# Moving the sink addition and the reciprocal of the softmax sums from VectorE to GpSimd

## The chip, the cores and the metric

The kernel runs on one core of a Trainium2 chip. The metric is device time in microseconds (us) from one launch; lower is better. A core has TensorE (PE; its weight loads are shown apart, as PEld), VectorE (DVE), ScalarE (ACT), GpSimd (POOL) and SyncE (SP), which here only issues DMAs. Each engine works through its own list of instructions in order, and waits at the head of the list for semaphores that other engines raise.

## The reference

Two layers over 512 tokens of width 1024. Each layer normalises its input, projects it, runs two branches and projects back. One branch is a gated linear recurrence (HGRN2), the other a sliding-window attention of 16 heads with a learned sink per head. Only the softmax of the attention matters here:

```python
s = jnp.where(mask, q_k_scores * ATT_SCALE, NEG_INF)        # (heads, 128 queries, 256 keys)
sink = broadcast(sinks)                                     # one logit more per head
p = jax.nn.softmax(jnp.concatenate([s, sink], axis=-1), axis=-1)[..., :-1]
o = jnp.einsum('bnkgqs,bnskd->bnqkgd', p, vw)
```

The sink's exponential therefore enters the sum that divides each row, and nothing else.

## The kernel before, in words

The work of a layer is a long list of projections (line L302: each 128x512 product is made of three matmuls, from a high and a low part of activations and weights), and beside them the attention and the recurrence. Weights arrive by DMA as `raw`; ACT copies out the high part (L189) and DVE subtracts it to get the low part `wlo` (L190).

The attention of a layer is 16 steps, one for each block `n` of 128 queries (4) and each group `g` of four heads (4). `att_stream` starts in turn i the scores of step i (`att_scores`), the transposes of step i-2 (`att_transpose`), and the products with V of step i-4 (`att_value`). `merge` interleaves these turns with projection steps in the text of the program. In a step:

- PE makes the scores into PSUM (`sc`, L560 for n = 0, L573 otherwise). DVE masks them (L564, L578), takes the row maximum (L566, L580), and forms the negated bound `negm` (L584) and the sink's exponent `ds` (L587).
- ACT takes four exponentials of 128x128 into `pt` (tile `s`), and accumulates each row's sum into a column of `sums`, 128x4 (L591). It then takes the exponential of the sink, `es`, 128x4 (L594).
- DVE adds `es` to `sums` (L595) and takes the reciprocal in place (L596).
- GpSimd multiplies the 128x512 tile `pt` by the reciprocals (L598).
- Two turns later PE transposes `pt` (L604). ACT and DVE split the transposes into a high and a low part in tile `a` (L350, L351). For n > 0 GpSimd cuts the two halves of the window out of them with two affine selects (L616, tiles `pcur` or `b`, and `pprev`). PE multiplies with V (L630), ACT and DVE fold the result (L632, L636).

GpSimd has other work in the same stretch: the last rotations of q (L524, L525) at its start, and the memset and products of the recurrence's preparation (L725, L743) at its end.

The order of the instructions on each engine is fixed when the program is built. Instructions given to `pin` keep the order of the text among themselves; scores, transposes and V products are pinned. All others, the projections' matmuls (L302) of this stretch and the instructions of DVE, ACT and GpSimd in `att_scores` among them, are ordered by a list scheduler with its own estimate of times. A few DVE instructions are raised by `tc.high_priority(300)`: mask, maximum, `negm` and `ds`. The addition and the reciprocal are not raised.

GpSimd already takes powers elsewhere: `rstd_of` computes an inverse square root of a 128x4 tile by a one-input addition (L355) and a power with a tile of -0.5, `mhalf` (L357); `power` does so for 128x1 (L371), and the start of the kernel once for `rcol` (L1180, L1181).

Of the kernel before, what the change touches and what calls it, by code (L numbers as in the profile page):

```python
# [10 lines left out]
F32 = mybir.dt.float32  # L11
# [3 lines left out]
ALU = mybir.AluOpType  # L15
# [62 lines left out]
def hybrid_kernel(ctx: ExitStack, tc: tile.TileContext, x, xt, wkv, win, wout, g_pre, g_post, lbp, ghead, sinks,  # L78
                  gcol_c, cos_f, sin_f, cos_t, sin_t, masks_c, out):
    nc = tc.nc  # L80
    P = 128
    const = ctx.enter_context(tc.tile_pool(name="const", bufs=1))
# [8 lines left out]
    def pin(ins):  # L91
        return tc.keep_in_program_order(ins)
# [8 lines left out]
    def sc():  # L101
        sc_turn[0] += 1
        return sc_tiles[sc_turn[0] % SC]
# [5 lines left out]
    def tmp(tag, dt=F32, n=1):  # L109

        t = tp.tile([P, n, 512] if n > 1 else [P, 512], dt, tag=tag, name=tag, bufs=TB[tag])
        return t
# [316 lines left out]
    def layer(l, last):  # L429
# [119 lines left out]
        def att_scores(g, n):  # L549
            v = g // 2  # L550
            q = qs[g]
            hs = slice(4 * g, 4 * g + 4)
            t_ = slice(n * P, (n + 1) * P)
            mx_ = sm.tile([P, 4], F32, tag="mx", name="mx")
            cur = []
            if n == 0:
                S = sc()
                for h in range(4):
                    for p in range(2):
                        pin(nc.tensor.matmul(S[:, h * P:(h + 1) * P], lhsT=q[:, h, t_], rhs=kst[v][p][:, 0:P],  # L560
                                         start=(h == 0 and p == 0), stop=(h == 3 and p == 1)))
                Sv = S.rearrange("p (h s) -> p h s", h=4)
                with tc.high_priority(300):
                    nc.vector.copy_predicated(Sv, am4, neg.unsqueeze(2).broadcast_to([P, 4, P]))  # L564
                with tc.high_priority(300):
                    nc.vector.tensor_reduce(mx_, Sv, axis=AX.X, op=ALU.max)  # L566
                cur = [Sv[:, h, :] for h in range(4)]
            else:
                for hp_ in range(2):
                    S = sc()  # L570
                    for h in range(2):
                        for p in range(2):
                            pin(nc.tensor.matmul(S[:, h * 256:(h + 1) * 256], lhsT=q[:, 2 * hp_ + h, t_],  # L573
                                             rhs=kst[v][p][:, (n - 1) * P:(n + 1) * P],
                                             start=(h == 0 and p == 0), stop=(h == 1 and p == 1)))
                    Sv = S.rearrange("p (h s) -> p h s", h=2)
                    with tc.high_priority(300):
                        nc.vector.copy_predicated(Sv[:, :, P:2 * P], am2, Sv[:, :, 0:P])  # L578
                    with tc.high_priority(300):
                        nc.vector.tensor_reduce(mx_[:, 2 * hp_:2 * hp_ + 2], Sv[:, :, P:2 * P], axis=AX.X, op=ALU.max)  # L580
                    cur += [Sv[:, h, P:2 * P] for h in range(2)]
            negm = sm.tile([P, 4], F32, tag="negm", name="negm")
            with tc.high_priority(300):
                nc.vector.scalar_tensor_tensor(negm, mx_, -SCALE, nsnk[:, l, hs], op0=ALU.mult, op1=ALU.min)  # L584
            ds_ = sm.tile([P, 4], F32, tag="ds", name="ds")
            with tc.high_priority(300):
                nc.vector.tensor_tensor(ds_, snk[:, l, hs], negm, op=ALU.add)  # L587
            pt = tmp("s")
            sums = sm.tile([P, 4], F32, tag="sums", name="sums")
            for h in range(4):  # L590
                nc.scalar.activation(pt[:, h * P:(h + 1) * P], cur[h], AF.Exp, bias=negm[:, h:h + 1], scale=SCALE,  # L591
                                     accum_out=sums[:, h:h + 1])
            es = sm.tile([P, 4], F32, tag="es", name="es")
            nc.scalar.activation(es, ds_, AF.Exp)  # L594
            nc.vector.tensor_tensor(sums, sums, es, op=ALU.add)  # L595
            nc.vector.reciprocal(sums, sums)  # L596
            pv = pt.rearrange("p (h s) -> p h s", h=4)
            nc.gpsimd.tensor_tensor(pv, pv, sums.unsqueeze(2).broadcast_to([P, 4, P]), op=ALU.mult)  # L598
            return pt
# [38 lines left out]
        def att_stream(steps):  # L638


            pts, terms = {}, {}
            n = len(steps)
            for tt in range(NT):
                ensure(("k", l, tt))
            for i in range(n + VLAG):
                todo = []
                if i < n:
                    todo.append(lambda: pts.update({i: att_scores(*steps[i])}))
                if 2 <= i <= n + 1:
                    todo.append(lambda: terms.update({i - 2: att_transpose(*steps[i - 2], pts.pop(i - 2), i % 2)}))  # L650
                if i >= VLAG:
                    todo.append(lambda: att_value(*steps[i - VLAG], terms.pop(i - VLAG)))
                for fn in todo:
                    fn()
                    yield (SLOW[1] if i < SLOW[0] else 1.0) / len(todo)

                if i < n and steps[i][1] == NT - 1 and steps[i][0] < 2:
                    until(lambda: steps[i][0] + 2 in stacks)
                    load_q(steps[i][0] + 2)
# [442 lines left out]
    nc.gpsimd.affine_select(out=ident, in_=ident, pattern=[[-1, P]], compare_op=ALU.is_equal, fill=0.0, base=0, channel_multiplier=1)  # L1102
    mhalf = const.tile([P, 4], F32, name="mhalf")
    nc.vector.memset(mhalf, -0.5)
    first = sm.tile([P, 4], F32, tag="hr", name="first")
    nc.scalar.activation(first, mhalf, AF.Square)
    ones = tmp("u")
# [207 lines left out]
```

## Time and profile before

| | |
|---|---|
| median of 3 runs | 903.64 us (903.24 to 903.84) |
| the profiled execution | 904.02 us |
| its span, first to last instruction | 902.3 us |
| busy: PE, PEld, DVE, ACT, POOL | 99%, 83%, 72%, 52%, 28% |
| attention of the first layer | about 58 to 166 us |
| attention of the second layer | about 500 to 610 us |

In the lines of the profile, "out<-in" names the tiles an instruction writes and reads. A group's line gives the count, the busy time and the mean duration in ns, and then the idle time of its engine just before it with what ended it. A row of the timeline gives start and duration in us, engine, line, operation and tiles, and in square brackets the idle time before it and its releaser. A row of the waits reads "who <- whom: us in total, times, longest".

### The profile page before, as it was taken

The page shows a single profiled execution, that of the slowest core. Times are in us where ns is not written, and L with a number is a line of the kernel's source. Part 1 is how long each engine was busy: PE and PEld are TensorE (multiplying, and loading weights), DVE is VectorE, ACT ScalarE, POOL GpSimd, SP SyncE. Part 2 cuts the span into 40 slices and gives each one's busy share as a digit, 9 for nine tenths or more (in the row PEclk, how much of TensorE's full clock was granted, in tenths as well). Part 3 has the DMA queues.
Part 4 walks back from the last instruction along what each step waited for, and adds up shares of the span by engine and source line. Part 5 has one row for each costly group of instructions (what it writes and reads, how often), then busy time and mean ns, then how long its engine had stood idle before and what let it go on. Part 6 is the DMA issues. An engine that isn't in the chain of part 4 may idle for free.

```text
span 902.3 us, 18581 instructions
## 1 busy us (share of the span) xinstructions
PE 893.0 (99%) x7206; PEld 747.7 (83%) x7206; DVE 650.7 (72%) x1179; ACT 472.3 (52%) x1067; POOL 256.5 (28%) x233
## 2 busy tenths in 40 slices
PE   9999999999999999999999999999999999999996
PEld 7888888888888888888898888888888888888885
DVE  5888987989666785555777787877767558666556
ACT  6536767754665323534464376686356463145242
POOL 0135445204313123021332344450124121330102
PEclk9999999999999999999999999999999999999999
DMA  9683712322222222434347455222322322223413
GB/s 307 222 225 117 211 46 72 105 94 80 77 82 70 94 82 63 128 119 132 116 153 217 128 164 163 71 80 76 115 72 61 105 71 86 70 73 93 140 36 140
DMA packets 57144, 102.82 MB, mean 114 GB/s; under 512 B 6624, under 2 KB 9184, under 8 KB 57056
## 3 DMA queue, kind: packets, MB, share of 16 engines
q1 hardware_dynamic: 56768, 101.50, 37.2%
q8 instruction: 57, 0.93, 0.4%
q14 instruction: 31, 0.25, 0.1%
q10 hardware_dynamic: 288, 0.14, 0.1%
HBM read 89.03 MB, written 12.58 MB: 113 GB/s over the span
## 4 chain that ended last, share of the span: by engine, by line
PE 95%; DVE 3%; ACT 1%; issue 0%; POOL 0%; POOLq 0%; DVEq 0%; ACTq 0%
PE pj L302 77%; PE ac L630 3%; PE sc L573 2%; PE sc L771 2%; PE ac L840 2%; PE ac L1140 1%; PE sc L604 1%; PE ac L843 1%; PE ac L827 1%; PE sc L902 1%; PE sc L815 1%; PE ac L712 1%; PE sc L560 1%; PE sc L1117 1%; DVE wlo L190 0%; PE sc L775 0%
## 5 line engine op out<-in xcount | busy, mean ns | idle before, releaser
L189 ACT CAST whi<-raw 128x512 fp32r<-128x512 f32 x256 | 155.5, 621 | 126.9 <-PE pj L302 113.4
L190 DVE TENSOR_TENSOR wlo<-raw,whi 128x512 fp32r<-128x512 f32 x253 | 184.1, 746 | 43.4 <-ACT whi L189 42.3
L302 PE MATMUL pj<-hhi,wlo 128*128 128x512 f32 x512 | 202.4, 396 | 0.0
L302 PE MATMUL pj<-hhi,whi 128*128 128x512 f32 x512 | 199.9, 390 | 0.0
L302 PE MATMUL pj<-hlo,whi 128*128 128x512 f32 x512 | 199.4, 389 | 0.0
L302 PE MATMUL pj<-whi,ops 128*128 128x512 f32 (+1 forms) x520 | 172.1, 395 | 0.0
L302 PEld LDWEIGHTS pj<-whi,ops 128*128 128x128 f32 x520 | 97.2, 188 | 19.6 <-DVE y L925 0.3
L302 PEld LDWEIGHTS pj<-hhi,whi 128*128 128x128 f32 x512 | 96.1, 188 | 20.6
L302 PEld LDWEIGHTS pj<-hhi,wlo 128*128 128x128 f32 x512 | 96.2, 188 | 19.3
L302 PEld LDWEIGHTS pj<-hlo,whi 128*128 128x128 f32 x512 | 96.3, 188 | 18.9
L302 PE MATMUL pj<-whi,hlo 128*128 128x512 f32 x256 | 102.9, 404 | 0.0
L302 PE MATMUL pj<-wlo,ops 128*128 128x512 f32 (+1 forms) x260 | 100.7, 387 | 0.0
L302 PE MATMUL pj<-wlo,hhi 128*128 128x512 f32 x256 | 100.1, 391 | 0.3 <-DVE wlo L190 0.3
L302 PE MATMUL pj<-whi,hhi 128*128 128x512 f32 x256 | 100.2, 391 | 0.0
L790 POOL TENSOR_TENSOR k<-k,tot 128x512 f32<-128x512 f32 x40 | 58.0, 1473 | 107.5 <-PE sc L771 51.8
L591 ACT ACTIVATE s<-sc,negm 128x128 f32<-128x128 f32 x128 | 45.6, 370 | 33.4 <-DVE negm L584 25.7
L302 PEld LDWEIGHTS pj<-whi,hhi 128*128 128x128 f32 x256 | 48.0, 188 | 10.3
L302 PEld LDWEIGHTS pj<-wlo,ops 128*128 128x128 f32 x260 | 49.0, 188 | 8.8
L302 PEld LDWEIGHTS pj<-wlo,hhi 128*128 128x128 f32 x256 | 48.3, 189 | 8.7 <-DVE wlo L190 0.8
L302 PEld LDWEIGHTS pj<-whi,hlo 128*128 128x128 f32 x256 | 48.2, 188 | 8.0
L789 DVE TENSOR_TENSOR q<-q,tot 128x512 f32<-128x512 f32 x40 | 37.6, 951 | 20.4 <-PE sc L775 10.9
L598 POOL TENSOR_TENSOR s<-s,sums 128x512 f32<-128x512 f32 x32 | 34.7, 1084 | 52.6 <-DVE sums L596 32.2
(223 smaller groups left out, 1391.4 us busy)
## 6 DMA issues: line engine op xcount, KB each, us to landing
raw<-in_win_dram SPq DMA_DIRECT2D x192, 256.0 KB, 2.7
raw<-in_wout_dram SPq DMA_DIRECT2D x64, 256.0 KB, 2.7
stack<-rot SPq DMA_DIRECT2D x16, 512.0 KB, 3.9
qs<-stack SPq DMA_DIRECT2D x32, 256.0 KB, 4.4
xs<-in_xt_dram SPq DMA_DIRECT2D x8, 256.0 KB, 4.8
raw<-in_wkv_dram SPq DMA_DIRECT2D x8, 256.0 KB, 3.7
a<-in_x_dram SPq DMA_DIRECT2D x8, 256.0 KB, 3.3
x_mid<-a SPq DMA_DIRECT2D x8, 256.0 KB, 2.2
```

Source lines behind the costliest of these rows:

```text
L189: keep(nc.scalar.copy(hi, v))
L190: keep((nc.gpsimd if i in on_pool and i % 2 else nc.vector).tensor_tensor(lo, v, hi.bitcast(F32), op=ALU.subtract))
L302: ins = nc.tensor.matmul(u.o, lhsT=u.sta(k, u.w)[i], rhs=u.mov(k, u.w)[j], start=(n == 0), stop=(n == len(u.list) - 1))
L560: pin(nc.tensor.matmul(S[:, h * P:(h + 1) * P], lhsT=q[:, h, t_], rhs=kst[v][p][:, 0:P], start=(h == 0 and p == 0), stop=(h == 3 and p == 1)))
L573: pin(nc.tensor.matmul(S[:, h * 256:(h + 1) * 256], lhsT=q[:, 2 * hp_ + h, t_], rhs=kst[v][p][:, (n - 1) * P:(n + 1) * P], start=(h == 0 a ...
L591: nc.scalar.activation(pt[:, h * P:(h + 1) * P], cur[h], AF.Exp, bias=negm[:, h:h + 1], scale=SCALE, accum_out=sums[:, h:h + 1])
L598: nc.gpsimd.tensor_tensor(pv, pv, sums.unsqueeze(2).broadcast_to([P, 4, P]), op=ALU.mult)
L630: pin(nc.tensor.matmul(U, lhsT=vst[v][:, blk, :], rhs=d, start=(i == 0), stop=(i == len(terms) - 1)))
L771: pin(nc.tensor.matmul(L[32 * b:32 * b + 32, c:c + 16], lhsT=k[:, o_ + 32 * b:o_ + 32 * b + 32], rhs=qv[:, blk:blk + qu, 1, :], start=True ...
L789: nc.vector.tensor_tensor(qv[:, :, 1, :], qv[:, :, 1, :], tv[:, :, 0].unsqueeze(2).broadcast_to([P, 2 * nb, hh]), op=ALU.mult)
L790: nc.gpsimd.tensor_tensor(kv_[:, :, 0, :], kv_[:, :, 0, :], tv[:, :, 1].unsqueeze(2).broadcast_to([P, 2 * nb, hh]), op=ALU.mult)
L840: pin(nc.tensor.matmul(O[:, c], lhsT=A[:, c], rhs=vs(j, n), start=(n == 0), stop=False))
```

## The change

The addition of the sink's exponential moves from DVE to GpSimd. The reciprocal becomes a power with an exponent of -1 on GpSimd, with the exponent read from a new constant tile `mone` of 128x4. Both stand directly ahead of GpSimd's scaling of the same step. The constant is filled once by GpSimd, right after the making of the identity at the start of the kernel.

```diff
             nc.scalar.activation(es, ds_, AF.Exp)
-            nc.vector.tensor_tensor(sums, sums, es, op=ALU.add)
-            nc.vector.reciprocal(sums, sums)
+            nc.gpsimd.tensor_tensor(sums, sums, es, op=ALU.add)
+            nc.gpsimd.tensor_tensor(sums, sums, mone, op=ALU.pow)
             pv = pt.rearrange("p (h s) -> p h s", h=4)
             nc.gpsimd.tensor_tensor(pv, pv, sums.unsqueeze(2).broadcast_to([P, 4, P]), op=ALU.mult)
...
     nc.vector.memset(mhalf, -0.5)
+    mone = const.tile([P, 4], F32, name="mone")
+    nc.gpsimd.memset(mone, -1.0)
```

## The prediction

> **What bounds the kernel now.** I read the page from the top first: span, busy shares, and the chain that ended last.
>
> ```profile
> span 902.3 us, 18581 instructions
> PE 893.0 (99%) x7206; PEld 747.7 (83%) x7206; DVE 650.7 (72%) x1179; ACT 472.3 (52%) x1067; POOL 256.5 (28%) x233
> PE 95%; DVE 3%; ACT 1%; issue 0%; POOL 0%; POOLq 0%; DVEq 0%; ACTq 0%
> ```
>
> PE is busy for 893.0 of 902.3 us, and 95% of the chain is its own work. GpSimd has no share of it. So time can be won only from PE's few gaps, and lost only where something makes PE wait longer. Next, the two stretches that hold all 32 attention steps, and the busiest part of the first one for DVE (columns: stretch, PE, PEld, DVE, ACT, POOL busy, clock, DMA share, GB/s).
>
> ```profile
> 58.00:166.00 108.00, 107.76 (x561) 89.79 (x560) 89.66 (x208) 72.61 (x226) 51.13 (x47) 1.00 0.41 116
> 500.00:610.00 110.00, 109.48 (x570) 91.63 (x568) 90.36 (x208) 74.39 (x231) 53.84 (x48) 1.00 0.41 115
> 85.00:110.00 25.00, 24.76 (x131) 20.29 (x132) 24.48 (x60) 19.00 (x60) 12.67 (x13) 1.00 0.72 196
> ```
>
> In 218 us of attention PE idles 0.24 + 0.52 = 0.76 us. GpSimd is busy for 51.13 + 53.84 = 105.0 us, less than half. DVE is nearly full (24.48 of 25 us) between 85 and 110. Then the waits that touch the moved work, and the three of PE and PEld that DVE or ACT end in these stretches.
>
> ```profile
> POOL s L598 <- DVE sums L596: 32.2, 15, 6.7
> DVE sums L595 <- ACT es L594: 13.1, 13, 1.6
> PEld sc L604 <- POOL s L598: 0.4, 1, 0.4
> PEld sc L573 <- ACT s L591: 3.9, 14, 0.6
> PE sc L573 <- ACT s L591: 0.4, 2, 0.2
> PE pj L302 <- DVE wlo L190: 0.3, 1, 0.3
> ACT s L591 <- DVE negm L584: 25.7, 18, 4.2
> ```
>
> The transposes read what GpSimd scales, and in 32 steps they waited for it once, for 0.4 us. That is the line that carries the forecast: the moved work lies two turns ahead of its reader.
>
> **The change part by part.**
>
> *DVE loses two instructions a step.*
>
> ```profile
> L595 DVE TENSOR_TENSOR sums<-sums,es 128x4 f32<-128x4 f32 x32 | 10.1, 316 | 13.1 <-ACT es L594 13.1
> L596 DVE RECIPROCAL sums<-sums 128x4 f32<-128x4 f32 x32 | 5.6, 175 | 0.8
> L355 POOL TENSOR_SCALAR hr<-hss 128x4 f32<-128x4 f32 x16 | 3.9, 246 | 114.7 <-DVE hss L848 114.7
> L357 POOL TENSOR_TENSOR hrr<-hr,mhalf 128x4 f32<-128x4 f32 x16 | 16.2, 1014 | 1.3
> 268.09 0.20 POOL L355 TENSOR_SCALAR hr<-hss 128x4 f32<-128x4 f32 x1 [13.48 <-DVE hss L848]
> 268.37 1.03 POOL L357 TENSOR_TENSOR hrr<-hr,mhalf 128x4 f32<-128x4 f32 x1
> ```
>
> DVE is relieved of 10.1 + 5.6 = 15.7 us of work, and of 13.1 us in which it stood at the addition until ACT had the sink's exponential. This is not on the path, but what it may bring there is bounded by PE's waits for DVE and ACT: 0.76 us of idle time shows, and if every weight-load wait for L591 were lost to PE in full, 3.9 us more. The gain is between 0 and 4.7 us. I take 0.3, near the lower end: the weight load runs ahead of the matmuls, so that of those 3.9 us only the row of 0.4 us is seen to stop PE itself, and ACT waits there for `negm`, which is at raised priority already.
>
> *GpSimd gains two.* The power has an exact precedent, 128x4 with a constant tile: 1014 ns. The two-input addition of 128x4 is not in the trace. The nearest row is the one-input operation on 128x4 just quoted (0.20 us alone, and 0.28 us from its start to that of the power). The next two-input row is this one:
>
> ```profile
> L743 POOL TENSOR_TENSOR k<-k,f x16: 848/859/1429, 156.9 to 736.2; 128x256 f32<-128x256 f32 x16
> L355 POOL TENSOR_SCALAR hr<-hss x16: 194/194/565, 268.1 to 848.7; 128x4 f32<-128x4 f32 x16
> ```
>
> So the addition lies between 0.20 and 0.86 us; I take 0.2, since 128x256 has 64 times the elements. The scaling then starts 0.28 + 1.03 = 1.31 us after the addition could, and at worst 0.93 + 1.4 = 2.3 us (0.86 for the addition with its hand-over, and a power held up as much as the longest L355, 0.37 us more than its median). Over 32 steps GpSimd gains 42 us: 147 of 218 us of attention, still with room.
>
> *What that does to the scaling.* Before, the addition and the reciprocal stood in DVE's queue, so the scaling came much later than two short instructions would say. Here are the steps in which the reader follows most closely, with the sink's exponential where it matters, the scaling, and the transposes that read it (for the second step of these also GpSimd's work just ahead):
>
> ```profile
> 63.04 0.21 ACT L594 ACTIVATE es<-ds 128x4 f32<-128x4 f32 x1
> 64.79 1.04 POOL L598 TENSOR_TENSOR s<-s,sums 128x512 f32<-128x512 f32 x1 [6.69 <-DVE sums L596]
> 66.29 0.59 PEld L604 LDWEIGHTS sc<-ident,s 128*128 128x128 f32 x4
> 84.33 1.09 POOL L616 TENSOR_SCALAR_AFFINE_SELECT pprev<-a 128x1024 fp32r<-128x1024 f32 x1
> 84.76 0.21 ACT L594 ACTIVATE es<-ds 128x4 f32<-128x4 f32 x1
> 85.82 1.04 POOL L598 TENSOR_TENSOR s<-s,sums 128x512 f32<-128x512 f32 x1 [0.40 <-DVE sums L596]
> 86.92 0.57 PEld L604 LDWEIGHTS sc<-ident,s 128*128 128x128 f32 x4
> 90.23 0.22 ACT L594 ACTIVATE es<-ds 128x4 f32<-128x4 f32 x1
> 92.76 1.04 POOL L598 TENSOR_TENSOR s<-s,sums 128x512 f32<-128x512 f32 x1 [3.80 <-DVE sums L596]
> 93.85 0.20 PEld L604 LDWEIGHTS sc<-ident,s 128*128 128x128 f32 x2 [0.40 <-POOL s L598]
> 102.45 1.04 POOL L598 TENSOR_TENSOR s<-s,sums 128x512 f32<-128x512 f32 x1 [1.00 <-DVE sums L596]
> 105.40 0.60 PE L604 MATMUL sc<-ident,s 128*128 128x128 f32 x4
> 147.74 1.04 POOL L598 TENSOR_TENSOR s<-s,sums 128x512 f32<-128x512 f32 x1
> 151.25 0.59 PEld L604 LDWEIGHTS sc<-ident,s 128*128 128x128 f32 x4
> ```
>
> The step at 84.76: the exponential ends at 84.97, the scaling began at 85.82. Now GpSimd is free at 85.42, and the scaling begins at about 85.45 + 1.31 = 86.76, 0.95 us later. Its reader was ready 0.06 us after its end, so PE waits about 0.9 us. The step at 90.23: the exponential ends at 90.45, GpSimd is idle, and the scaling begins at 90.5 + 1.31 = 91.8 instead of 92.76, so 0.95 us earlier; the one wait of 0.4 us goes. The first step of all: the exponential ends at 63.25, so the scaling begins at 63.3 + 1.31 = 64.6 instead of 64.79: nothing. The step at 102.45 ends at 103.49, 1.9 us ahead of the transposes at 105.40, more than the whole 1.31. Of the other 28 steps the closest is the one at 147.74: it ends at 148.78, 2.5 us ahead of 151.25. These are covered by PE's projections in between; without that cover a step would cost up to 1.31 us.
>
> *What is queued behind on GpSimd.* The addition waits for ACT at the head of the queue, but the scaling waited in the same place for something that came later, so the wait is not longer, only 1.31 us of work is added. Behind it come the affine selects of the step before last, which PE's V products read. The tightest pair has no addition ahead of it:
>
> ```profile
> 80.42 1.10 POOL L616 TENSOR_SCALAR_AFFINE_SELECT pcur<-a 128x1024 fp32r<-128x1024 f32 x1 [5.13 <-DVE a L351]
> 83.19 0.39 PE L630 MATMUL ac<-pcur,vst 128*128 128x512 f32 x1
> 24.12 0.24 POOL L1180 TENSOR_SCALAR t<-ss 128x4 f32<-128x4 f32 x1 [22.77 <-ACT x L1167]
> 24.45 1.05 POOL L1181 TENSOR_TENSOR rcol<-t,mhalf 128x4 f32<-128x4 f32 x1
> 24.58 0.69 DVE L190 TENSOR_TENSOR wlo<-raw,whi 128x512 fp32r<-128x512 f32 x1 [2.93 <-ACT whi L189]
> ```
>
> GpSimd idled 5.13 us ahead of it. Other V products follow their selects by several us, so 1.31 us more is covered. The new constant costs a memset ahead of 22.77 us in which GpSimd idles: nothing. No DMA is issued or moved, and SP's queue is untouched.
>
> *Whether the power holds DVE up.* In the last two rows a power ran from 24.45 to 25.50, and a DVE subtraction with both inputs in SBUF began inside it and took 0.69 us, no longer than elsewhere. So I charge DVE nothing. The Trainium skill ("SBUF — State Buffer", section "Who interferes with whom") says that a DVE instruction with two SBUF inputs and a GpSimd instruction that reads SBUF lock each other out for the whole instruction. By that rule the subtraction would have begun at 25.50; this row does not bear it out for a power, and the sum by the rule is the rival priced below.
>
> *The sum*, against the profiled execution's own 904.02 us: +0.9 (step at 84.76) - 0.1 (of the 0.4 us of weight-load wait, what PE itself lost: 93.85 is 0.05 us after the scaling's end) - 0.3 (relief of DVE) = +0.5, so 904.5; this execution stood 0.38 us above the median, so 904.1 in terms of the median. With the bounds: at the upper price of 2.3 us the step at 84.76 costs 1.9 us and the first step 63.3 + 2.3 - 64.79 - 0.46 = 0.35 us, which gives 905.8 without any relief; with 4.7 us of relief and one slow step it is 899.7.
>
> **The rivals.**
>
> *Slower: transposes placed too near (13%).* The order of projections around the transposes is made anew at the build. If the scheduler takes the GpSimd pair for cheaper than 1.31 us, more steps look like the one at 84.76, each costing PE up to 0.95 us. For: two steps were placed within 0.1 us. Against: apart from four of the first eight steps of the first layer, 2.5 us or more lie between. It decides from three such steps; with four, 903.64 + 4 x 0.95 = 907.4 us.
>
> *Slower: GpSimd's power shuts DVE out (3%).* Between 85 and 110, with DVE nearly full, five steps would each cost DVE up to 1.01 us and return 0.32 + 0.18 = 0.5 us, so PE would wait for `wlo` some 5 x 0.5 = 2.5 us: 906.1 us. The row at 24.58 speaks against it. The mechanism is that of the Trainium skill's rule above.
>
> *Faster: DVE's relief reaches PE (12%).* DVE no longer stands waiting for ACT, masks and maxima run earlier, ACT frees the score banks earlier, and the waits of L573 and of L302 on `wlo` go. It needs over 1.8 us of the 4.7 that I bounded; with 2.5 us and no slow step 903.64 - 2.5 = 901.1 us. Against: only 0.76 us is visible as PE idling.
>
> **How the numbers follow.** Hidden as described has 72%, with its own range 902.4 to 905.3. About 0.2%, 1.8 us, is what a measurement of this kernel can tell from no change. Faster by more: 12%; slower by more: 13 + 3 = 16%; the rest is the same. The range that leaves out some 2 in 10 is 902.0 to 906.3.
>
> **What would show it.** In the changed profile the addition should take about 0.2 us and the power 1.01; GpSimd's busy time should be near 256.5 + 40 = 297 us and DVE's near 635. PE's busy time should stay at 893. PEld's wait at L604 for L598 should stay within about 1.5 us over all steps, and L190's mean of 746 ns should not rise. The forecast is wrong if the transposes wait in several steps, if V products begin to wait for affine selects, or if the power is much longer than 1.01 us.

## The result and the profile after

The changed kernel takes 908.63 us (median; 908.17 to 908.90) beside 903.54 us for the kernel before on the same chip. The ratio is 1.0055, 95% interval 1.004 to 1.007. It is slower by about 5 us; the forecast was 904.1 us, with 902.0 to 906.3 as its range.

First the page of the kernel after: span, busy shares, and the shares of the chain that ended last.

```profile
span 906.8 us, 18553 instructions
PE 893.9 (99%) x7206; PEld 747.1 (82%) x7206; DVE 650.5 (72%) x1115; ACT 473.6 (52%) x1067; POOL 298.1 (33%) x298
PE 90%; DVE 5%; ACT 2%; DMA 1%; issue 1%; POOL 0%; POOLq 0%; DVEq 0%; SPq 0%; ACTq 0%
```

The span grew by 4.5 us. PE's busy time grew by 0.9 and its idle time from 902.3 - 893.0 = 9.3 to 906.8 - 893.9 = 12.9 us, so by 3.6. The second thing to see is in the chain: GpSimd, which was given the work, still has 0% of it. DVE, which was relieved, went from 3% to 5%. And DVE's busy time is 650.5 us as before (650.7), though 64 instructions worth 15.7 us have left it.

The two attention windows of the kernel after, with the same columns as before:

```profile
58.00:166.00 108.00, 106.18 (x550) 87.71 (x549) 88.81 (x175) 72.84 (x226) 71.81 (x78) 1.00 0.40 114
500.00:610.00 110.00, 107.46 (x558) 89.68 (x557) 84.86 (x170) 70.53 (x223) 72.89 (x78) 1.00 0.39 114
```

PE now idles 1.82 + 2.54 = 4.36 us there, against 0.76: the whole 3.6 us. The granted clock is 1.00 in both. Next the waits of the kernel after that touch the attention ("who <- whom: total, times, longest"):

```profile
PE sc L573 <- ACT s L591: 2.8, 6, 0.6
PEld sc L573 <- ACT s L591: 7.1, 15, 1.0
PE pj L302 <- DVE wlo L190: 1.0, 1, 1.0
PE sc L604 <- POOL s L598: 0.6, 1, 0.6
PEld sc L604 <- POOL s L598: 1.3, 2, 1.0
ACT s L591 <- DVE negm L584: 33.7, 19, 4.8
```

Only 0.6 us of PE's waiting is for GpSimd's scaling, the only wait that the prediction charged. The larger part is the scores of the next step (L573). They wait until ACT has emptied the score bank (L591), and ACT waits for the bound `negm` from DVE. In the kernel before, that first row read 0.4 us, and the row of ACT 25.7.

What made DVE late can be seen in the means of its groups: first of the kernel before, then of the kernel after.

```profile
L190 DVE TENSOR_TENSOR wlo<-raw,whi 128x512 fp32r<-128x512 f32 x253 | 184.1, 746 | 43.4 <-ACT whi L189 42.3
L584 DVE SCALAR_TENSOR_TENSOR negm<-mx,nsnk 128x4 f32<-128x4 f32 x32 | 7.7, 241 | 0.4
L587 DVE TENSOR_TENSOR ds<-snk,negm 128x4 f32<-128x4 f32 x32 | 11.9, 373 | 0.6
```

```profile
L190 DVE TENSOR_TENSOR wlo<-raw,whi 128x512 fp32r<-128x512 f32 x253 | 190.7, 772 | 42.7 <-ACT whi L189 41.4
L584 DVE SCALAR_TENSOR_TENSOR negm<-mx,nsnk 128x4 f32<-128x4 f32 x32 | 11.4, 355 | 0.5
L587 DVE TENSOR_TENSOR ds<-snk,negm 128x4 f32<-128x4 f32 x32 | 14.3, 446 | 0.7
```

The same instructions take longer: 6.6 + 3.7 + 2.4 = 12.7 us more in these three groups. A wait inside an instruction shows as duration, not as idle time, so it stands in no row of waits; I call an instruction that waits in this way held. One place shows how it comes about. The timeline of the kernel after:

```profile
136.89 1.09 POOL L616 TENSOR_SCALAR_AFFINE_SELECT pprev<-a 128x1024 fp32r<-128x1024 f32 x1
137.13 1.39 DVE L190 TENSOR_TENSOR wlo<-raw,whi 128x512 fp32r<-128x512 f32 x1
137.95 1.44 POOL L596 TENSOR_TENSOR sums<-sums,mone 128x4 f32<-128x4 f32 x1
137.96 0.60 PE L604 MATMUL sc<-ident,s 128*128 128x128 f32 x4
139.46 1.04 POOL L598 TENSOR_TENSOR s<-s,sums 128x512 f32<-128x512 f32 x1
139.77 1.28 DVE L190 TENSOR_TENSOR wlo<-raw,whi 128x512 fp32r<-128x512 f32 x1
140.97 0.15 DVE L584 SCALAR_TENSOR_TENSOR negm<-mx,nsnk 128x4 f32<-128x4 f32 x1
141.16 0.37 ACT L591 ACTIVATE s<-sc,negm 128x128 f32<-128x128 f32 x1 [1.93 <-DVE negm L584]
142.02 1.44 PE L573 MATMUL sc<-kst,qs 128*128 128x256 f32 x8 [0.47 <-ACT s L591]
```

and the same place in the kernel before:

```profile
136.81 1.57 POOL L598 TENSOR_TENSOR s<-s,sums 128x512 f32<-128x512 f32 x1
136.97 0.60 PE L604 MATMUL sc<-ident,s 128*128 128x128 f32 x4
138.73 0.68 DVE L190 TENSOR_TENSOR wlo<-raw,whi 128x512 fp32r<-128x512 f32 x1
139.33 0.15 DVE L584 SCALAR_TENSOR_TENSOR negm<-mx,nsnk 128x4 f32<-128x4 f32 x1
140.40 1.41 PE L573 MATMUL sc<-kst,qs 128*128 128x256 f32 x8
```

Before, the scaling ended at 138.38 and the subtraction at 138.73 took 0.68 us. By its transposes (L604) the kernel after already runs 0.99 us late here, so I count from them. The subtraction that stands ahead of `negm` keeps its place, 1.81 us behind the transposes against 1.76. GpSimd's own work pushes the scaling from 0.16 us ahead of them to 1.50 us behind. So the subtraction starts inside the scaling and ends at 141.05, 0.55 us behind it; the one at 137.13 ended 0.54 us behind the select that it met. `negm` starts 3.01 us behind the transposes instead of 2.36, and PE stands 0.47 us at its scores, where it stood for none before. The second kind of place holds the bound itself (kernel after):

```profile
108.36 1.04 POOL L598 TENSOR_TENSOR s<-s,sums 128x512 f32<-128x512 f32 x1
109.35 1.09 POOL L616 TENSOR_SCALAR_AFFINE_SELECT pcur<-a 128x1024 fp32r<-128x1024 f32 x1
109.46 1.00 DVE L584 SCALAR_TENSOR_TENSOR negm<-mx,nsnk 128x4 f32<-128x4 f32 x1
110.49 0.37 ACT L591 ACTIVATE s<-sc,negm 128x128 f32<-128x128 f32 x1 [3.36 <-DVE negm L584]
111.35 0.74 PE L573 MATMUL sc<-kst,qs 128*128 128x256 f32 x4 [0.56 <-ACT s L591]
```

A 0.15 us instruction took 1.00 us, to the end of the select that had begun 0.11 us before it. The same place in the kernel before:

```profile
108.71 1.04 POOL L598 TENSOR_TENSOR s<-s,sums 128x512 f32<-128x512 f32 x1 [1.80 <-DVE sums L596]
109.48 0.29 DVE L584 SCALAR_TENSOR_TENSOR negm<-mx,nsnk 128x4 f32<-128x4 f32 x1
109.71 1.09 POOL L616 TENSOR_SCALAR_AFFINE_SELECT pcur<-a 128x1024 fp32r<-128x1024 f32 x1
```

There the select came 0.23 us behind the bound, and the bound took 0.29 us, to the end of the scaling at 109.75. PE's longest wait in the attention of the kernel after, 0.95 us for `wlo` at 522.44, is of this kind too: GpSimd's rotation L524 holds the bound for 0.71 us, where it took 0.15 before, and PE waited 0.34 us.

### The profile page after: what moved, and what is told of

Its sections match the earlier page's. It is cut to its first block, busy times and chain, and to the rows that moved or that the text cites. A ratio compares the mean times of both kernels' runs of the same rounds, so it can differ in the third digit from the quotient of the medians.

```text
span 906.8 us, 18553 instructions
## 1 busy us (share of the span) xinstructions
PE 893.9 (99%) x7206; PEld 747.1 (82%) x7206; DVE 650.5 (72%) x1115; ACT 473.6 (52%) x1067; POOL 298.1 (33%) x298
## 4 chain that ended last, share of the span: by engine, by line
PE 90%; DVE 5%; ACT 2%; DMA 1%; issue 1%; POOL 0%; POOLq 0%; DVEq 0%; SPq 0%; ACTq 0%
PE pj L302 73%; PE sc L771 2%; PE sc L573 2%; PE ac L630 2%; PE ac L840 2%; DVE wlo L190 1%; ACT s L591 1%; PE ac L1142 1%; PE ac L843 1%; PE ac L827 1%; PE sc L604 1%; PE sc L902 1%; DVE negm L584 1%; PE sc L815 1%; DVE sc L578 1%
## 5 line engine op out<-in xcount | busy, mean ns | idle before, releaser
L190 DVE TENSOR_TENSOR wlo<-raw,whi 128x512 fp32r<-128x512 f32 x253 | 190.7, 772 | 42.7 <-ACT whi L189 41.4
L591 ACT ACTIVATE s<-sc,negm 128x128 f32<-128x128 f32 x128 | 45.6, 369 | 42.2 <-DVE negm L584 33.7
L790 POOL TENSOR_TENSOR k<-k,f 128x512 f32<-128x512 f32 x8 | 15.3, 1936 | 86.0 <-PE sc L771 66.2
```

The costliest lines, as they stand in the source:

```text
L190: keep((nc.gpsimd if i in on_pool and i % 2 else nc.vector).tensor_tensor(lo, v, hi.bitcast(F32), op=ALU.subtract))
L790: nc.gpsimd.tensor_tensor(kv_[:, :, 0, :], kv_[:, :, 0, :], tv[:, :, 1].unsqueeze(2).broadcast_to([P, 2 * nb, hh]), op=ALU.mult)
```

## The experiments

My theory after this comparison: the added GpSimd work moves later scalings and selects onto DVE instructions that lead to `negm`; these are held to the end of GpSimd's instruction, `negm` is late, ACT empties the bank late, and PE waits at L573. The rivals: the new order of instructions costs the time; the power itself shuts DVE out; or DVE only lacks slack. Each run was timed beside the kernel before, which had a median of 903.4 to 903.7 us each time.

**Is it the order?** PE's list in the kernel after differs from the one before by the places of two projection matmuls; those of the other engines differ more. `short_power` keeps every instruction of the kernel after in its place, but the power is a multiplication. The reciprocal is left out.

```diff
-            nc.gpsimd.tensor_tensor(sums, sums, mone, op=ALU.pow)
+            nc.gpsimd.tensor_tensor(sums, sums, mone, op=ALU.mult)
```

> The changed kernel with GpSimd's power replaced by a multiplication with the same constant tile (a reciprocal is left out; the output is not the reference's). Every engine's list of instructions has the same order as in the changed kernel; only GpSimd's second small instruction should be near 0.2 us instead of 1.01. Three theories. SHIFT: GpSimd's longer chain pushes the scaling and the affine selects to later times, where they meet DVE's instructions with two SBUF inputs ahead of negm, so DVE, ACT and at last PE's scores wait: 903.5 to 905.5 us here, PE's waits at L573 back to under 1 us. ORDER: the loss comes from the new order of DVE and ACT, or from the loss of the two DVE instructions: 908 to 909 us. POWER: the power itself keeps DVE from its operands while it runs: 903.5 to 905.5 us.

Measured: 904.07 us, ratio 1.0005 (0.9996 to 1.0014). `power_beside` is the other half: DVE keeps its addition and reciprocal, so the order of PE, DVE and ACT is that of the kernel before, and GpSimd takes a power with exponent +1 between the reciprocal and the scaling.

```diff
             nc.vector.reciprocal(sums, sums)
+            nc.gpsimd.tensor_tensor(sums, sums, mone, op=ALU.pow)
```

> The kernel before, with addition and reciprocal left on DVE, and a power with exponent 1 added on GpSimd ahead of the scaling. PE, DVE and ACT have the same order as in the kernel before. GpSimd's part of a step is 1.1 us longer and starts after DVE's. SHIFT: 907 to 912 us. ORDER: 903.3 to 904.5 us, as before. POWER: 907 to 912 us.

Measured: 910.48 us, ratio 1.0078 (1.0065 to 1.0092). With the new order and a short instruction the loss is gone; with the old order and a long one it is larger than the change's. The order falls as a cause. In `power_beside` the chain has one link more (DVE's reciprocal ends, then GpSimd's power, then the scaling), and the transposes wait for it too, as its waits show:

```profile
PE sc L573 <- ACT s L591: 2.9, 5, 0.8
PE sc L605 <- POOL s L599: 2.1, 3, 1.1
```

Its bounds are held no longer than in the kernel before (228 ns in the mean against 241), so little of its loss can pass through them. The longest of its waits at the scores, 0.84 us at 143.8, comes behind a subtraction that took 1.29 us under the scaling.

**Is it the power, or any work of its length?** `fill_for_power` puts four memsets of 128x128 in place of the power. They take about as long, but read nothing. The reciprocal and the addition's result are left out: the scaling multiplies by 1.

```diff
-            nc.gpsimd.tensor_tensor(sums, sums, es, op=ALU.add)
-            nc.gpsimd.tensor_tensor(sums, sums, mone, op=ALU.pow)
+            nc.gpsimd.tensor_tensor(fill[:, 0:4], sums, es, op=ALU.add)
+            for _ in range(4):
+                nc.gpsimd.memset(fill, 1.0)
```

> The changed kernel with the power replaced by four GpSimd memsets of 128x128 (the scaling is by 1; a reciprocal is left out). DVE, ACT and PE keep the order of the changed kernel; GpSimd is held for about the same 1 us a step by instructions that read nothing. SHIFT: 907 to 909.5 us, as slow as the changed kernel. ORDER: 908 to 909 us. POWER: 903.5 to 905.5 us, since nothing reads SBUF on GpSimd in that time.

Measured: 906.37 us, ratio 1.0032 (1.0021 to 1.0044), below the 907 to 909.5 that I had expected. The group of the memsets and PE's wait at the scores in that run:

```profile
L598 POOL MEMSET fill<- 128x128 f32 x128 | 26.2, 205 | 6.9
PE sc L573 <- ACT s L591: 1.2, 3, 0.5
```

Work that reads nothing, 4 x 0.205 = 0.82 us a step, costs 2.7 us of the 5: moving GpSimd's later work is enough for about half of the loss. The rest, 2.3 us, goes with the power alone, and its length does not explain it. Where nothing stands in the way, the scaling begins 1.47 us behind the sink's exponential with the memsets and 1.44 with the power; over 32 steps it is 2.23 against 2.17 us in the mean. But three waits of PE in the kernel after are missing with the memsets: 0.47 us at 142.0, 0.61 at 554.2 and 0.47 at 591.0. Two of them, the first and the last, come behind a power that DVE held in its turn (1.44 us where 1.01 is the rule, as in the row at 137.95), and the scaling behind it begins 0.5 us later than with the memsets. It matters which scalings are late, not how late they are in the mean.

**One part alone.** `add_only` leaves the reciprocal on DVE, `power_only` leaves the addition there.

```diff
             nc.gpsimd.tensor_tensor(sums, sums, es, op=ALU.add)
-            nc.gpsimd.tensor_tensor(sums, sums, mone, op=ALU.pow)
+            nc.vector.reciprocal(sums, sums)
```

> Half of the change: only the addition moves to GpSimd, the reciprocal stays on DVE. GpSimd gains 0.28 us a step in place of 1.31, but the step crosses from GpSimd to DVE and back. SHIFT: 903.3 to 905 us. If the addition's move is what costs: 906 to 909 us.

```diff
-            nc.gpsimd.tensor_tensor(sums, sums, es, op=ALU.add)
+            nc.vector.tensor_tensor(sums, sums, es, op=ALU.add)
             nc.gpsimd.tensor_tensor(sums, sums, mone, op=ALU.pow)
```

> The other half of the change: the addition stays on DVE, the reciprocal becomes GpSimd's power. GpSimd gains about 1.0 us a step. SHIFT: 906.5 to 910 us, most of the loss or all of it. If the loss needed both halves together: under 905.5 us.

Measured: 905.42 us for the addition alone, ratio 1.0020 (1.0011 to 1.0029), and 907.15 us for the power alone, 1.0041 (1.0028 to 1.0055). The power is the costly part. The addition alone came out between my theory's range (903.3 to 905) and the rival's (906 to 909). Of its 1.8 us, most is one wait at the end of the first layer's attention, which the kernel after does not have (waits of `add_only`):

```profile
PE ac L630 <- DVE oa L636: 1.2, 1, 1.2
```

**Which held instruction carries it?** First, both kernels with the bound's inputs moved: for n > 0 the maxima go to a dead corner of the score bank in PSUM, and the bound is formed from there, in halves. The whole reference is computed.

```diff
-                        nc.vector.tensor_reduce(mx_[:, 2 * hp_:2 * hp_ + 2], Sv[:, :, P:2 * P], axis=AX.X, op=ALU.max)
+                        nc.vector.tensor_reduce(S[:, 0:2], Sv[:, :, P:2 * P], axis=AX.X, op=ALU.max)
+                        nc.vector.scalar_tensor_tensor(negm[:, 2 * hp_:2 * hp_ + 2], S[:, 0:2], -SCALE, nsnk[:, l, h0:h0 + 2],
+                                                       op0=ALU.mult, op1=ALU.min)
```

> The changed kernel, with the row maxima of n > 0 written to a dead part of the score bank in PSUM, and negm formed for each half from there, so that negm has one SBUF input instead of two. SHIFT: part of the loss returns, since negm itself no longer waits for GpSimd, while L190 ahead of it still can: 904.5 to 907.5 us. ORDER: not told apart, the order on DVE is new. POWER: 906 to 908.6 us.

> The kernel before, with the maxima of n > 0 in PSUM and negm formed for each half from there, as tried on the changed kernel. SHIFT: the two gaps of the kernel before that hang on L591 (0.50 us near 106 and 0.34 near 527) shrink: 902.3 to 903.6 us. If the gain on the changed kernel was only that of a new order: 902.5 to 905 us.

Measured: 904.33 us on the kernel after, ratio 1.0010 (1.0001 to 1.0019), and 904.07 us on the kernel before, 1.0005 (0.9996 to 1.0014). The difference between the two shrinks from 5.1 to 0.3 us. The bound's group in that version of the kernel after, with its shortest, median and longest duration in ns:

```profile
L584 DVE SCALAR_TENSOR_TENSOR negm<-sc,nsnk x48: 141/152/161, 61.9 to 591.6; 128x2 f32<-128x2 f32 x48
```

None of 48 was held. But the edit also splits the bound, so that ACT may start on two heads earlier, and it moves some 50 rows of PE's order. The kernel before with it missed my theory's 902.3 to 903.6 us and lies in the range that I gave for a mere new order (902.5 to 905), so this pair doesn't exclude that rival. So I freed the bound in two ways that split nothing. `after_bound_one_input` forms it by an instruction with one input, without the sinks:

```diff
-                nc.vector.scalar_tensor_tensor(negm, mx_, -SCALE, nsnk[:, l, hs], op0=ALU.mult, op1=ALU.min)
+                nc.vector.tensor_scalar(negm, mx_, -SCALE, 0.0, op0=ALU.mult, op1=ALU.min)
```

> The kernel after, with one edit: the negated bound negm is formed by an instruction with one input in SBUF (the maxima, against a constant of 0), where the original reads the maxima and the sinks. The sink's part of the bound is left out. The instructions of PE, ACT and GpSimd stand in the same order as in the kernel after but for one projection matmul, the count of DVE's is unchanged, and DVE is relieved of nothing but what the instruction waited inside itself. Theory: GpSimd's shifted scalings and selects hold DVE's instructions with two SBUF inputs, and the bound is one of those held (1.00 us at 109.46 us, instead of 0.15). Then every bound takes 0.2 us or less, the gaps that follow a held bound (at about 110, 521 and 553 us, together some 2 us) go, and those that follow a held subtraction L190 (at about 141, 559 and 590 us) stay: 906 to 907.5 us. If only the subtractions matter, nothing changes: 908.2 to 909. Rival: what helped in the two earlier edits was not the lock but slack on DVE or an earlier start of ACT's exponentials, neither of which this edit gives: 908.2 to 909 as well, even though the bound is short.

Measured: 908.78 us, ratio 1.0059 (1.0045 to 1.0073), no better. Its group shows why this says nothing about the theory:

```profile
L584 DVE TENSOR_SCALAR negm<-mx 128x4 f32<-128x4 f32 x32 | 11.2, 351 | 0.5
```

I had taken one input for free, and it is held like the original (351 against 355 ns). A tensor reduce is not held, so the next pair forms the bound by one over the maxima. The scale, the sign and the sinks' part are left out of the bound. On both kernels the order of PE, ACT, GpSimd and SP stays, instruction for instruction.

```diff
-                nc.vector.scalar_tensor_tensor(negm, mx_, -SCALE, nsnk[:, l, hs], op0=ALU.mult, op1=ALU.min)
+                nc.vector.tensor_reduce(negm, mx_.unsqueeze(2), axis=AX.X, op=ALU.max)
```

> The kernel after, with the negated bound negm formed by a tensor reduce over the maxima (the scale, the sign and the sink's part of the bound are left out). In the runs so far DVE's reduce with one SBUF input was never held by GpSimd (679 ns for each L190), where a one-input tensor_scalar was held like the original (mean 351 ns against 355). The orders on PE, ACT, GpSimd and SP are those of the kernel after, instruction for instruction. Theory (a held bound is itself one link of the loss): every bound takes about 0.15 us, the gaps of 0.72 and 0.77 us at about 110 and 553 us go, and the one of 1.11 at 521 us shrinks; those behind a held subtraction (141, 559, 590 us) stay: 906 to 907.5 us. Rival (only the subtractions L190 matter, or slack on DVE): 908.2 to 909.

> The kernel before with the same edit of the bound (same parts left out, orders on PE, ACT, GpSimd and SP those of the kernel before). All theories: the few held bounds of the kernel before cost PE nothing, so 903.2 to 904; it is the partner of the run with the same edit on the kernel after.

Measured: 905.08 us on the kernel after, ratio 1.0014 (1.0006 to 1.0023), and 902.85 us on the kernel before, 0.9989 (0.9980 to 0.9997). Both came out below what I had expected: 3.5 us for the kernel after instead of 1 to 2.5, and 0.8 us for the kernel before, where I expected nothing. The group, the wait of PE and the place at about 110 us, all of `after_bound_reduce`:

```profile
L584 DVE TENSOR_REDUCE negm<-mx 128x4 f32<-128x4 f32 x32 | 4.8, 150 | 0.5
```

```profile
PE sc L573 <- ACT s L591: 0.7, 2, 0.5
```

```profile
110.06 1.09 POOL L616 TENSOR_SCALAR_AFFINE_SELECT pcur<-a 128x1024 fp32r<-128x1024 f32 x1
110.17 0.16 DVE L584 TENSOR_REDUCE negm<-mx 128x4 f32<-128x4 f32 x1
110.36 0.37 ACT L591 ACTIVATE s<-sc,negm 128x128 f32<-128x128 f32 x1 [2.50 <-DVE negm L584]
```

The select again begins 0.11 us ahead of the bound, and the bound takes 0.16 us. PE's wait for L591 falls from 2.8 to 0.7 us. This is the cleanest of the runs: one form of a small instruction, nothing else moved, and 2.9 of the 5.1 us between the two kernels go. Two waits that I had expected to stay went as well. The subtraction ahead of the bound is still held, 1.28 us at 138.99, and so is its twin at 585.81, yet PE no longer waits at the scores that follow. At the first of them DVE is further ahead of PE: the subtraction begins 1.15 us behind the transposes, where it was 1.81. So here a held subtraction cost PE time only where DVE had no such lead.

**The subtractions.** On both kernels, L190 on DVE becomes a reduce that reads one input. The low parts are left out.

```diff
+                keep(nc.vector.tensor_reduce(lo, hi.bitcast(F32).unsqueeze(2), axis=AX.X, op=ALU.max))
```

> The changed kernel with the same one-input L190 (the low parts of the weights are left out). SHIFT, with DVE's two-input instructions as what GpSimd's later work collides with: of the eight gaps of over 0.25 us on PE in the changed kernel those behind a stretched L190 go (near 141, 521, 559 and 590 us, 0.6 to 1.1 us each), those behind GpSimd's scaling itself (near 86) and behind negm's own wait (near 110 and 553) stay: 1.5 to 3 us above the run with the kernel before, instead of 4.9. If collisions on L190 play no part and DVE, ACT or GpSimd are late for another reason: 4 to 5.5 us above it.

> The kernel before, with DVE's L190 changed from a subtraction of two SBUF tiles to a reduction over an axis of length 1 that reads only the high part (the low parts of the weights are left out, so the output is not the reference's). It is the base for the next run: L190 should now take 0.68 to 0.70 us wherever GpSimd is. All theories: 902.5 to 904.5 us.

Measured: 904.36 us after, ratio 1.0009 (1.0000 to 1.0018), and 901.70 us before, 0.9977 (0.9968 to 0.9985). The kernel before came out below the 902.5 to 904.5 that I had expected. Between them lie 2.7 us, where it was 5.1, with the same order on PE in both (it is a new one, some 60 rows of it moved in the kernel after and some 150 in the kernel before). Each L190 now takes the same time, as the group of the kernel after with this edit shows (shortest, median, longest in ns):

```profile
L193 DVE TENSOR_REDUCE wlo<-whi x253: 627/678/709, 13.8 to 872.8; 128x512 fp32r<-128x512 f32 x127
```

In the kernel after the median is 687 and the longest 1781 ns, so what the edit took away is the held ones. That also gives DVE 184.1 - 167.3 = 17 us of slack in the kernel before and 23 in the kernel after, and slack was a rival. The next pair was meant to give the time back: five of every eight reduces are followed by a small one on the raw weights.

```diff
+                if i % 8 < 5:
+                    scr = sm.tile([P, 4], F32, tag="scr", name="scr", bufs=1)
+                    keep(nc.vector.tensor_reduce(scr, v[:, 0:4].unsqueeze(2), axis=AX.X, op=ALU.max))
```

> The kernel after with the subtraction L190 replaced by the one-input reduce, as before (the low parts are left out), and now five of every eight followed by a small DVE reduce of 128x4 that reads the raw weights, so that DVE gets back about the time that it no longer waits, and the raw buffers are released as late as before. Theory (held instructions on DVE's way to negm): the waits are gone whatever DVE's load, so 904 to 905.5 us. Rival (the one-input form helped because it gave DVE 23 us of slack): with the slack taken back the time returns to 907.5 to 909.

> The kernel before with the same edit (low parts left out, five of every eight followed by the small reduce). It gives the partner for the difference: theory 902 to 903.5 us, with the after version some 2 to 3 us above it; rival, 903.5 to 904.5 us, with the after version 4 to 5 us above it.

Measured: 905.84 us after, ratio 1.0022 (1.0012 to 1.0031), and 905.16 us before, 1.0019 (1.0010 to 1.0028). The two groups of the kernel after with this edit add up to 192.2 us, about what L190 took in the kernel after (190.7):

```profile
L193 DVE TENSOR_REDUCE wlo<-whi 128x512 fp32r<-128x512 f32 x253 | 168.0, 679 | 42.6 <-ACT whi L189 41.2
L196 DVE TENSOR_REDUCE scr<-raw 128x4 f32<-128x4 f32 x160 | 24.2, 151 | 30.5 <-DMA raw<-in_win_dram 21.2 <-DMA raw<-in_wout_dram 8.2
```

But the small reduces overlap their neighbours. DVE's whole busy time is 633.6 us here, against 622.1 without them and 650.5 in the kernel after; for the kernel before it is 642.1, 630.2 and 650.7. So they gave back 11.5 of 28.4 us, and 11.9 of 20.5.

The kernel after stands 0.3 us above the theory's 905.5 and far below the rival's 907.5. The kernel before missed both expectations: the small reduces cost it 3.5 us (905.16 against 901.70), which no theory had. The difference of the pair is 0.7 us, not the 4 to 5 that lack of slack would have given, and below the 2 to 3 of my theory. The small reduces move PE's order against the pair without them, and most of the time was not given back, so this pair does not settle what slack is worth to either kernel. Against slack as the difference between the two kernels speaks that DVE has no less of it in the kernel after: in the two attention windows it is busy for 88.81 + 84.86 = 173.7 us, against 89.66 + 90.36 = 180.0 before.

Last, both edits together (maxima in PSUM, and L190 by the reduce).

> The changed kernel with both edits (the low parts of the weights are left out), so that on the way to negm for n > 0 no DVE instruction reads two SBUF tiles. SHIFT by collisions on DVE: what is left above the run with the kernel before is the direct wait of the transposes for the scaling (0.7 us) and the n = 0 steps: 0.3 to 1.8 us above it. If GpSimd's length costs PE in another way than through DVE: 2.5 to 5 us above it.

> The kernel before with both earlier edits: L190 reads one input (the low parts of the weights are left out) and the maxima of n > 0 go through PSUM. Base for the next run. 901 to 903 us.

Measured: 901.99 us after, ratio 0.9980 (0.9971 to 0.9989), and 901.21 us before, 0.9971 (0.9960 to 0.9981). The order of PE and ACT is the same in both. The pairs in one table, in us:

| freed from the hold | before | after | difference |
|---|---|---|---|
| nothing | 903.54 | 908.63 | 5.1 |
| the bound, by a reduce | 902.85 | 905.08 | 2.2 |
| the bound, through PSUM | 904.07 | 904.33 | 0.3 |
| the subtractions | 901.70 | 904.36 | 2.7 |
| the subtractions, DVE's time given back in part | 905.16 | 905.84 | 0.7 |
| the subtractions and the bound through PSUM | 901.21 | 901.99 | 0.8 |

The parts don't add up: the difference falls by 2.9 us with the bound, by 2.4 with the subtractions and by 4.3 with both. What is left is not the direct step at 86 us: with both edits PE never waits for the scaling. These are its waits at the scores in `after_no_lock`:

```profile
PE sc L577 <- ACT s L599: 0.6, 2, 0.5
```

The longer one, 0.46 us at 526.1, comes behind a bound of n = 0, which the edit leaves in its form; it took 0.94 us under a select.

That more than half of the loss hangs on the held bound is shown by the pair with the reduce, where every engine keeps its order. That most of the rest passes through other held instructions is argued from the places above and from the last pair; its edits also relieve DVE and move PE's order. How the loss divides between `negm` and the subtractions depends on the order of each build and stays open, and so does what slack on DVE is worth.

No kernel that leaves nothing out came out ahead of the kernel before.

## Why the prediction was wrong

*The prices of the instructions were right.* The addition was put at 0.2 us and the power at 1.01, and these are the medians of the kernel after (shortest, median, longest in ns):

```profile
L595 POOL TENSOR_TENSOR sums<-sums,es x32: 195/202/725, 62.7 to 597.0; 128x4 f32<-128x4 f32 x32
L596 POOL TENSOR_TENSOR sums<-sums,mone x32: 1006/1009/1631, 63.0 to 597.3; 128x4 f32<-128x4 f32 x32
```

GpSimd's busy time was put at 297 us and is 298.1; PE's at 893 and is 893.9.

*The one direct step was nearly right.* At 84.76 the scaling's delay was to cost PE 0.9 us. PE waited there:

```profile
87.21 0.55 PE L604 MATMUL sc<-ident,s 128*128 128x128 f32 x3 [0.56 <-POOL s L598]
```

By the distances between PE's starts about 0.7 us was lost. The transposes' weight loads waited 1.3 us in all, within the 1.5 allowed for.

*The step that failed is "So I charge DVE nothing".* "These are covered by PE's projections in between" held for what it speaks of: PE waits for the transposes' input in one step, and no V product waits for a select. But the work behind the addition on GpSimd was followed only to the instructions that read its results. The scalings, the selects and the rotations also hold DVE instructions that meet them, so moving them moves the holds. Charged at nothing, this came to 12.7 us more inside L190, L584 and L587; PE's wait at the scores rose from 0.4 to 2.8 us and its wait for `wlo` from 0.3 to 1.0. I had looked for a cover of data and not for a cover of DVE. The kernel before held the sign of it: its bound took 241 ns in the mean where its median was 155, and L587 373 where its median was 162.

The row at 24.58 was read rightly, and it showed only that a power already running did not hold DVE up. It did not speak of the scaling and the selects that come later, nor of a power that starts under a DVE instruction. The 0.3 us of relief failed with it: the 15.7 us that left DVE were used up inside L190, L584 and L587 and in others, so that DVE's time, which was to fall to 635 us, is 650.5. L190's mean was not to rise above 746 ns and is 772. Both are signs that the forecast had named.

*The order behind "directly ahead" was not kept.* In the built program a select stands between the addition and the power in six of 32 steps, as in the one at 136.89, so that the scaling came later than the 1.31 us assumed. By the trace the scalings begin 2.17 us behind the exponential's end in the mean over 32 steps, against 1.48 before.

*The rivals.* The rival of the transposes had the right sign but the wrong reader: PE waits at the transposes in one step, not in four. The 3% rival (GpSimd shuts DVE out, 906.1 us) had the right kind of mechanism. It put the hold on the power and the loss on `wlo`, and the runs show the scalings, selects and rotations behind it, and the loss mostly at L573 through `negm`. PE's wait for `wlo` is 1.0 us, 0.7 more than before. The Trainium skill ("SBUF — State Buffer", section "Who interferes with whom") has a DVE instruction with two SBUF inputs and a GpSimd instruction that reads SBUF exclude each other for a whole instruction. For the scaling and the selects this case agrees: 1.28 us at 139.77, 1.00 at 109.46, and no holds with one input in PSUM (48 bounds of 141 to 161 ns). It says there too that `tensor_scalar` can enter a mode that contends and `tensor_reduce` on this chip cannot; the 351 and 150 ns agree. For a power that is already running, the 0.69 us at 24.58 still speak against it, and so does the kernel after: five subtractions that began 0.21 to 1.28 us into a power took 681 to 694 ns, as here.

```profile
107.27 1.01 POOL L596 TENSOR_TENSOR sums<-sums,mone 128x4 f32<-128x4 f32 x1
107.48 0.68 DVE L190 TENSOR_TENSOR wlo<-raw,whi 128x512 fp32r<-128x512 f32 x1
```

*The range's upper end, 906.3,* came from readers of the scaling alone. With a term for the 2.4 us by which PE's wait at the scores rose, it would have held the time.

## What to carry to other kernels

When work is added to an engine that is half idle, don't look only at who reads its results: list what comes later on that engine, and which instructions of the neighbour it will now meet. Mean durations well above the median of the same instruction can be waits that no row of waits shows; find which of them stand ahead of the bound engine, here a 0.15 us instruction that ACT and PE depend on. Look for a form of that instruction that isn't held, and price it as a change of its own. Here the reduce brought 0.8 us on the kernel before, but it leaves out parts of the bound; the form through PSUM computes the whole bound and brought nothing there (904.07 us).

## What the runs showed of the hardware

- A one-input `tensor_scalar` on 128x4 in SBUF was held by GpSimd just as its two-input form (mean 351 against 355 ns, longest about 1.0 us). A `tensor_reduce` of the same tile (136 to 159 ns) and a two-input form with one input in PSUM (141 to 161 ns) were not held once in these runs.
- The hold goes both ways. The power took 1.44 us at 137.95, under a DVE subtraction that had begun at 137.13 and ended at 138.52: from there to its end at 139.39 are 0.87 us, so most of its 1.01 us came after it. A power that was already running held none of the subtractions that began inside it.
- GpSimd memsets, which read nothing, still cost 2.7 us in `fill_for_power`, by what they moved.
- The price is not in proportion to the added work: two instructions of 0.20 us a step cost 0.4 us in all (`short_power`, within its interval of none), and one of 0.20 with one of 1.01 us about 5.
